# Sums of the way back's weights formed during the way in of a two-layer MLP, and the first loads of the way back asked for earlier

## The chip, the cores and the metric

The kernel runs on one core of one Trainium2 chip. The metric is the device time of one execution in microseconds; the number compared is the median of several executions.

## The reference

Two blocks work on a sequence of 1024 tokens of width 1024, in float32. The first has a mixer, an MLP and a gated addition; the second has a gated MLP, attention beside a state-space mixer, and a second gated MLP. What matters here are the three MLPs:

```python
# first block, MLP: 1024 -> 4096 -> 1024
z = rms_norm(h, norm_mlp_g[l])
h = h + jnp.square(jax.nn.relu(z @ w_up[l])) @ w_down[l]
# second block, twice: 1024 -> 2 x 2816, gated, -> 1024
def swiglu(x, w_in, w_out):
    gate, up = jnp.split(x @ w_in, 2, axis=-1)
    return (jax.nn.silu(gate) * up) @ w_out
```

## The kernel before, in words

**Products.** Each large product is made by Strassen's scheme in Winograd's form: both factors are cut into 2x2 blocks, and seven products of sums of blocks replace eight. Each factor of such a product is split into a float32r high part and a low part (on ScalarE the high part, on VectorE or GpSimd the low one), and three matmuls (high by high, high by low, low by high) stand for one.

**The way in** (`ups_s`, L526 to L606) makes z times the first weight. It goes over pairs of column pieces, numbered n: 16 pairs in the MLP, 22 in each gated one. z's right-hand factors are kept in SBUF as 28 tiles of the tag `u`, which has 32 buffers. A pair's left factors are made by `lefts` (L493 to L517): two `raw` loads of 512 KB, sums on VectorE (L505, L506, L507, L515), splits by `factor`. The pool `raw` (L306) has two buffers, and its loads are kept in program order (`last_raw`, L309 to L311), all on SyncE's queue. For n from 3 on the loop L593 to L604 runs the products p2(n), p3(n-1), p1(n), p4(n-1), asks for the left factors of n+1 (L599), calls `also`, and runs p6(n), p5(n), p7(n); one product is 12 matmuls of 128x512. `use` takes finished quarters through the nonlinearity, and `lay_by` (L608 to L624) forms the sums of h that the way back needs as its left factors and stores them in DRAM (`hs`). The tag `s`, four buffers, holds `st` of `lefts`, and in the MLP also the tiles `hz` and `hw` of `lay_by`.

**The way back** (`down_s`, L645 to L767) makes h times the second weight. It goes over units (p, q): p is one of seven products in the order 2, 1, 5, 3, 6, 7, 4, and q a quarter of the inner dimension (8 of them in the MLP, 6 in the gated ones, the last one half as large). A unit (L691) loads a left factor `sd` from `hs` and a right factor, splits both (L687, L688) into tiles `wh`, `wl`, `tt`, and runs 24 matmuls (L701). A load is put in the schedule behind the end of the unit four units back (`ends`, L661).

**Right factors.** Four of the seven right factors are sums of blocks of the second weight. In the two gated MLPs `rights` (L626 to L637) forms them during the way in: two `raw` loads (`x`, `y`), four subtractions on VectorE (L635), two stores to `tw` in DRAM (L637); the way back loads them from there (`td`). `also` (L1171) spreads the 11 calls over 19 steps. In the MLP there is no `tw`: `right` (L664) loads blocks of `w_down` (`wd`), 64 loads of 512 KB, eight of them a second block for p = 7, and subtracts in place on VectorE (L669) before the split, for p = 5, 6, 7 and 4; the first block stays in the `u` pool (`W`) over several products.

**What sets the order.** Each engine, and SyncE's queue of loads and stores, runs its instructions in the order that the compiler's scheduler wrote down. `after` (L299) adds an ordering to that scheduler alone, without a semaphore. A queue entry that waits holds up all behind it. `aside` hangs other work on given units of the way back: the constants and eighths of the state-space mixer (`s5_small`, `s5_eighth`) and, on unit (7, 4), `ple_in` (L999), which loads the input of the next stage into `raw`. `fetch` (L342) loads the next stage's weights through the same two `raw` buffers.

Of the kernel before, what the change touches and what calls it, by code (L numbers as in the profile page):

```python
# [15 lines left out]
ALU = mybir.AluOpType  # L16
PSUM = bass.MemoryType.PSUM
DRAM = bass.MemoryType.DRAM
P = 128
# [3 lines left out]
H = 512  # L23
# [224 lines left out]
class Model:  # L248
    def __init__(self, ctx, tc, a, out):
        self.tc, self.nc, self.a, self.out = tc, tc.nc, a, out  # L250
        pool = lambda n, b, **k: ctx.enter_context(tc.tile_pool(name=n, bufs=b, **k))
        self.pc = pool("c", 1)
        self.pu = pool("u", 32)
        self.pw = pool("w", NW)
        self.pr = pool("r", 2)
        self.pt = pool("t", 5)
        self.psm = pool("sm", 8)
        self.pd = pool("d", 1, space=DRAM)
        self.last_raw = None
        self.ps = pool("ps", 8, space=PSUM)  # L260


# [79 lines left out]
    def fetch(self, src, k):  # L342
        nc = self.nc
        n = src.shape[-1]
        r = self.raw(src, [n])
        shape = [P, k, n // k] if k else [P, n]
        h = self.pw.tile(shape, F32R, name="wh", tag="wh")
        l = self.pw.tile(shape, F32R, name="wl", tag="wl")
        if k:
            r = r.rearrange("p (k f) -> p k f", k=k)  # L350
        nc.scalar.activation(h, r, AF.Copy)  # L351
        nc.gpsimd.tensor_tensor(l, r, h.bitcast(F32), op=ALU.subtract)  # L352
        return h, l
# [169 lines left out]
        self.pairs = pairs  # L523
        self.first = [self.left_first(pairs[n][0]) for n in range(self.EARLY)]

    def ups_s(self, z, use, also=None):  # L526

        nc = self.nc
        pairs, E = self.pairs, self.EARLY
        left, a, c, s2, s3 = dict(enumerate(self.first)), {}, {}, {}, {}

        def product(p, n, bank, start):
            for k in range(4):
                zh, zl = z(p, k)
                wh, wl = left[n][p][0][:, k, :], left[n][p][1][:, k, :]
                for i, (w, x) in enumerate(((wh, zh), (wh, zl), (wl, zh))):  # L540
                    self.mark = nc.tensor.matmul(bank, w, x, start=start and k == 0 and i == 0,  # L541
                                                 stop=k == 3 and i == 2, skip_group_check=True)

        def p2(n):
            b = c[n] = self.bank()
            product(2, n, b, True)

        def p1(n):
            a[n] = self.bank()
            product(1, n, a[n], True)  # L550
            self.late = self.mark
            s1 = self.tmp("s1c")
            nc.scalar.activation(s1, a[n], AF.Copy)
            use(n, (0, 0), c.pop(n), s1)

        def p5(n):
            c[n] = self.bank()
            product(5, n, c[n], True)

        def p6(n):  # L560
            product(6, n, a[n], False)
            s2[n] = self.pr.tile([P, 2, H], F32, name="s2", tag="xr")[:, 0]
            nc.scalar.activation(s2[n], a[n], AF.Copy)

        def p7(n):
            product(7, n, a[n], False)
            s3 = self.tmp("s3")
            nc.scalar.activation(s3, a[n], AF.Copy)
            use(n, (1, 1), c[n], s3)

        def p3(n):
            product(3, n, c[n], False)
            use(n, (0, 1), c[n], s2[n])

        def p4(n):
            product(4, n, a[n], False)
            use(n, (1, 0), a[n], None)
            for x in (left, a, c, s2):
                del x[n]

        z.ready(0)
        z.settle()
        for n in range(E):
            p2(n)
            p1(n)
        z.ready(1)
        for n in range(E):
            self.lefts(*pairs[n], left[n])
        left[E] = self.lefts(*pairs[E])
        for p, n in ((p5, 0), (p5, 1), (p6, 0), (p6, 1), (p7, 0), (p7, 1), (p3, 0), (p5, 2), (p4, 0), (p6, 2), (p3, 1),  # L590
                     (p7, 2), (p4, 1)):
            p(n)
        for n in range(E, len(pairs)):  # L593
            p2(n)
            p3(n - 1)
            p1(n)
            p4(n - 1)
            if n + 1 < len(pairs):
                left[n + 1] = self.lefts(*pairs[n + 1])  # L599
            if also:  # L600
                also(n - E, len(pairs) - E)
            p6(n)
            p5(n)
            p7(n)  # L604
        p3(n)
        p4(n)  # L606
# [19 lines left out]
    def rights(self, w, tw, d):  # L626
# [9 lines left out]
        for i, t in enumerate((x, y)):  # L636
            nc.sync.dma_start(out=tw[d // 2][2 * i : 2 * i + 2, d % 2].rearrange("i p f -> p i f"), in_=t)  # L637


    RIGHT = {5: 0, 7: 1, 4: 2, 6: 3}  # L640


    LEFT = {2: (0, 0), 1: (0, 1), 5: (1, 0), 3: (1, 1), 6: (2, 0), 7: (2, 1), 4: (3, 0)}

    def down_s(self, hs, w, Y, done, z=None, aside={}, tail=1, tw=None):  # L645

# [1 line left out]
        v = nc.vector  # L650
        npair = w.shape[1]
        qs = [(p, min(2, npair - p)) for p in range(0, npair, 2)]
        W = {}
        ends = [self.late]
        ahead = 4

        def load(name, src, q):
            n = qs[q][1]
            t = self.u(name, shape=[P, 2, H])
            d = nc.sync.dma_start(out=t[:, :n], in_=src.rearrange("c p f -> p c f"))  # L660
            self.after(d, ends[max(len(ends) - ahead, 0)])  # L661
            return t

        def right(p, q):  # L664
            k, n = qs[q]
            if tw and p in self.RIGHT:
                return load("td", tw[q][self.RIGHT[p], :n], q)
            block = lambda b: load("wd", w[b, k : k + n], q)
            sub = lambda o, x, y: v.tensor_tensor(o[:, :n], x[:, :n], y[:, :n], op=ALU.subtract)  # L669
            t = block({2: 2, 1: 0, 5: 1, 3: 3, 6: 3, 7: 3, 4: 2}[p])  # L670
            if tw or p in (2, 3):
                return t
            if p == 1:
                W[q] = t
            elif p in (5, 6):
                sub(W[q], t, W[q])
                return W[q]
            elif p == 7:
                sub(t, t, block(1))
            else:  # L680
                sub(t, t, W.pop(q))
            return t

        def pair(tags, x, n):
            hi, lo = (self.u("tt", F32R, [P, 2, H]) if tag == "u" else self.pw.tile([P, 2, H], F32R, name=tag, tag=tag)
                      for tag in tags)
            nc.scalar.activation(hi[:, :n], x[:, :n], AF.Copy)  # L687
            v.tensor_tensor(lo[:, :n], x[:, :n], hi.bitcast(F32)[:, :n], op=ALU.subtract)  # L688
            return hi, lo

        def unit(p, q):  # L691
            n = qs[q][1]
            g, i = self.LEFT[p]
            s = load("sd", hs[q][g][i, :n], q)
            return pair(("wh", "wl"), s, n), pair(("u", "u"), right(p, q), n)

        def mm(bank, un, c, t, start, stop):
            (sh, sl), (th, tl) = un
# [50 lines left out]
        b = four()  # L749
# [3 lines left out]
        c = four()  # L753
# [11 lines left out]
                z.ready(0)  # L765

        product(4, a, False, c21, rest)  # L767


    def pool_in(self, g, pp):  # L770
# [196 lines left out]
    def mlp(self, z, aside={}):  # L967
        nc = self.nc
        hs, xy = [], {}

        def use(n, quarter, bank, other):
            i, j = quarter
            if (n, j) not in xy:
                xy[n, j] = self.u("h", shape=[P, 2, H], tag="s" if (n, j) == (1, 1) else "u")
            o = xy[n, j][:, (1 - i) if j == 0 else i]
            if other is not None:
                nc.vector.tensor_tensor(o, bank, other, op=ALU.add)
                bank = o
            nc.scalar.activation(o, bank, AF.Relu)
            nc.scalar.activation(o, o, AF.Square)  # L980
            if quarter == (1, 0):
                self.lay_by(hs, n, xy.pop((n, 0)), xy.pop((n, 1)), "s")

        self.ups_s(z, use)
        Y = [None] * NT

        def first(t):
            r = self.raw(self.xm[t], name="xr", tag="xr", after=self.mark)
            nc.vector.tensor_tensor(Y[t], Y[t], r, op=ALU.add)
            return self.rstd(Y[t])  # L990

        done, z = self.follow("norm_ple_g", first, lambda t, r: (Y[t], r))
        aside = dict(aside)
        aside[7, 4] = [self.ple_in]
        self.down_s(hs, self.a["w_down"], Y, done, z, aside)
        self.resume()
        return Y, z

# [148 lines left out]
    def ffn(self, n, z, seam, aside={}):  # L1147
# [19 lines left out]
                self.lay_by(hs, d, X.pop((d, 0)), X.pop((d, 1)), "u")  # L1167

        w, tw = self.a["f%d_out" % n], []

        def also(k, of):  # L1171
            if (k + 1) * w.shape[1] // of > k * w.shape[1] // of:
                self.rights(w, tw, k * w.shape[1] // of)

        self.ups_s(z, use, also)
        Y = [None] * NT
        done, z = seam(Y)
        self.down_s(hs, w, Y, done, z, aside, 1 if z else 2, tw)
        return z

    def half_scale(self, row, name):
# [548 lines left out]
```

## Time and profile before

| | us |
|---|---|
| median of three executions | 3058.43 |
| lowest and highest | 3047.64, 3059.11 |
| the profiled execution, its own time | 3056.01 |
| its span, first to last instruction | 3054.2 |
| TensorE busy (matmuls) | 2828.5 |
| VectorE, ScalarE, GpSimd busy | 1797.1, 1320.1, 784.1 |

The times below are microseconds from the span's first instruction. PE is TensorE, DVE VectorE, ACT ScalarE, POOL GpSimd, and SP SyncE, whose queue issues the loads and stores (SPq). L701 is line 701 of the kernel. In a timeline a bracket gives the engine's idle time before the instruction and what ended it. PEclk is the share of TensorE's full clock that was granted: 1.00 is 2.4 GHz, half of it 1.2 GHz. Matmuls overlap, so one of 0.39 us follows the one before it after less than that.

### The profile page before, as it was taken

How to read it: one execution, taken by the hardware profiler on the slowest of the kernel's cores; microseconds unless marked ns; L12 is line 12 of the kernel's file. 1: busy time of each engine (PE TensorE's matmuls, PEld its weight loads, DVE VectorE, ACT ScalarE, POOL GpSimd, SP SyncE). 2: the span in 40 equal slices, each digit the busy share in tenths (PEclk: the TensorE clock that was granted, in tenths of full speed). 3: DMA queues.
4: the chain of work that ended last, by engine and by line, in shares of the span. 5: the costliest groups of instructions: out<-in, count | busy, mean ns of one | idle time of the engine just before them, and what ended most of it. 6: DMA issues, size and time to landing. Idle time of an engine off the chain costs nothing. (4 is left out here: it accounts for less than half of the span.)

```text
span 3054.2 us, 33886 instructions
## 1 busy us (share of the span) xinstructions
PE 2828.5 (93%) x12585; PEld 2303.4 (75%) x12585; DVE 1797.1 (59%) x2561; ACT 1320.1 (43%) x1921; POOL 784.1 (26%) x626
## 2 busy tenths in 40 slices
PE   8998999989979989999989999997789999998997
PEld 7777877767757867778777878886677778777776
DVE  4586655575767366666667561417735756565445
ACT  5446554442335473323324362236655533332343
POOL 3320222200211221111122041349854112111001
PEclk9999999999989999999999999999899899999999
DMA  4114344474466123454466562423113244446645
GB/s 145 57 47 138 131 145 152 156 259 160 166 233 220 56 90 106 153 164 151 164 222 237 207 222 81 155 83 111 42 49 131 87 152 159 159 153 207 225 160 200
DMA packets 198200, 452.93 MB, mean 148 GB/s; under 512 B 20533, under 2 KB 25233, under 8 KB 198033
## 3 DMA queue, kind: packets, MB, share of 16 engines
q1 hardware_dynamic: 193424, 433.97, 41.9%
q10 hardware_dynamic: 4608, 16.78, 1.4%
q8 instruction: 99, 1.62, 0.2%
q14 instruction: 69, 0.56, 0.1%
HBM read 316.51 MB, written 129.99 MB: 146 GB/s over the span
## 5 line engine op out<-in xcount | busy, mean ns | idle before, releaser
L701 PE MATMUL b<-tt,wh 128*128 128x512 f32 x2128 | 686.2, 403 | 74.0 <-ACT tt L687 64.4
L541 PE MATMUL b<-zh,wh 128*128 128x512 f32 x1680 | 646.9, 398 | 35.4 <-ACT wh L481 25.6
L541 PE MATMUL b<-zh,wl 128*128 128x512 f32 x1680 | 625.3, 393 | 4.5 <-ACT wl L511 4.0
L541 PE MATMUL b<-zl,wh 128*128 128x512 f32 x1560 | 615.2, 395 | 8.4 <-DVE zl L211 8.4
L701 PEld LDWEIGHTS b<-tt,wh 128*128 128x128 f32 x2128 | 409.3, 194 | 181.5 <-ACT tt L687 73.8
L701 PE MATMUL b<-tt,wl 128*128 128x512 f32 x1064 | 424.1, 399 | 0.0
L541 PEld LDWEIGHTS b<-zh,wh 128*128 128x128 f32 x1680 | 319.8, 191 | 123.9 <-ACT wh L481 38.8
L541 PEld LDWEIGHTS b<-zh,wl 128*128 128x128 f32 x1680 | 318.2, 190 | 75.5 <-ACT wl L511 6.7
L541 PEld LDWEIGHTS b<-zl,wh 128*128 128x128 f32 x1560 | 296.4, 190 | 73.9 <-DVE zl L211 13.4
L688 DVE TENSOR_TENSOR wl<-sd,wh 128x1024 fp32r<-128x1024 f32 x140 | 167.6, 1197 | 190.3 <-ACT wh L687 190.3
L482 POOL TENSOR_TENSOR wl<-raw,wh 128x1024 fp32r<-128x1024 f32 x51 | 123.3, 2418 | 526.1 <-ACT wh L481 486.6
L701 PEld LDWEIGHTS b<-tt,wl 128*128 128x128 f32 x1064 | 206.7, 194 | 43.6
L481 ACT ACTIVATE wh<-raw 128x1024 fp32r<-128x1024 f32 x120 | 127.2, 1060 | 238.4 <-DMA raw<-in_f_in 95.2
L352 POOL TENSOR_TENSOR wl<-raw,wh 128x1024 fp32r<-128x1024 f32 (+1 forms) x58 | 142.7, 2465 | 322.0 <-ACT wh L351 290.2
L687 ACT ACTIVATE wh<-sd 128x1024 fp32r<-128x1024 f32 x140 | 141.5, 1011 | 154.6 <-DMA sd<-hs 111.9
L383 POOL TENSOR_SCALAR v<-ss 128x1 f32<-128x1 f32 x80 | 47.9, 599 | 472.5 <-ACT junk L376 466.3
L619 POOL TENSOR_TENSOR hw<-h 128x512 f32<-128x512 f32 x38 | 60.2, 1583 | 421.1 <-DVE h L1165 188.1
L687 ACT ACTIVATE tt<-wd 128x1024 fp32r<-128x1024 f32 x92 | 94.6, 1028 | 150.3 <-DVE wd L669 133.1
L505 DVE TENSOR_TENSOR s<-raw 128x512 f32<-128x512 f32 x60 | 82.2, 1370 | 107.5 <-DMA raw<-in_f_in 100.6
L482 DVE TENSOR_TENSOR wl<-raw,wh 128x1024 fp32r<-128x1024 f32 x69 | 88.7, 1286 | 84.2 <-ACT wh L481 43.2
L351 ACT ACTIVATE wh<-raw 128x1024 fp32r<-128x1024 f32 (+1 forms) x58 | 59.5, 1031 | 168.2 <-issue 42.7
L688 DVE TENSOR_TENSOR tt<-wd,tt 128x1024 fp32r<-128x1024 f32 x92 | 110.2, 1198 | 27.6 <-ACT tt L687 26.8
(358 smaller groups left out, 5003.4 us busy)
## 6 DMA issues: line engine op xcount, KB each, us to landing
sd<-hs SPq DMA_DIRECT2D x126, 512.0 KB, 5.5
raw<-in_f_in SPq DMA_DIRECT2D x94, 512.0 KB, 3.7
wd<-in_w_down SPq DMA_DIRECT2D x64, 512.0 KB, 6.3
raw<-in_f_out SPq DMA_DIRECT2D x44, 512.0 KB, 3.6
tw<-raw SPq DMA_DIRECT2D x44, 512.0 KB, 2.9
td<-tw SPq DMA_DIRECT2D x40, 512.0 KB, 6.3
hs<-h SPq DMA_DIRECT2D x38, 512.0 KB, 3.1
hs<-hw SPq DMA_DIRECT2D x38, 512.0 KB, 3.0
```

The source lines that it names most:

```text
L351: nc.scalar.activation(h, r, AF.Copy)
L352: nc.gpsimd.tensor_tensor(l, r, h.bitcast(F32), op=ALU.subtract)
L383: nc.gpsimd.tensor_scalar(out=v, in0=ss, scalar1=1.0 / D, scalar2=EPS, op0=ALU.mult, op1=ALU.add)
L481: nc.scalar.activation(hi.rearrange("p a b -> p (a b)"), x, AF.Copy)
L482: eng.tensor_tensor(lo.rearrange("p a b -> p (a b)"), x, hi.bitcast(F32).rearrange("p a b -> p (a b)"), op=ALU.subtract)
L505: v.tensor_tensor(s1, a21, a22, op=ALU.add)
L541: self.mark = nc.tensor.matmul(bank, w, x, start=start and k == 0 and i == 0, stop=k == 3 and i == 2, skip_group_check=True)
L619: g.tensor_tensor(wt[:, 1], x[:, 1], y[:, 0], op=ALU.subtract)
L687: nc.scalar.activation(hi[:, :n], x[:, :n], AF.Copy)
L688: v.tensor_tensor(lo[:, :n], x[:, :n], hi.bitcast(F32)[:, :n], op=ALU.subtract)
L701: self.mark = nc.tensor.matmul(bank, x[:, c, ts], y[:, c], start=start and k == 0, stop=stop and k == 2, skip_group_check=True)
```

## The change

- The MLP gets `rights` too. `back` makes the hooks for all three MLPs: `also` now has all the sums done one step before the last (`of - 1`), so 16 calls over 12 steps in the MLP and 11 over 18 in the gated ones, and `down_s` has no other path: its right factors are `td` or an unchanged block `wd`.
- `last`, called once in the last pair behind p1(n), asks for the factors of units (2, 0) to (2, 3), eight tiles of the tag `u`, which `unit` then takes from `self.pre`.
- `fetch` is put in the schedule behind `self.gate`, the end of the fifth unit from the end of the way back that came last (unit (4, 3) in the MLP, (4, 1) in the first gated one).
- `ple_in` moves from unit (7, 4) to (7, 2).

```diff
@@ -342,7 +342,7 @@
     def fetch(self, src, k):
-        r = self.raw(src, [n])
+        r = self.raw(src, [n], after=self.gate)
@@ -594,11 +594,12 @@
             p2(n)
             p3(n - 1)
             p1(n)
+            if n + 1 == len(pairs):
+                last()
             p4(n - 1)
             if n + 1 < len(pairs):
                 left[n + 1] = self.lefts(*pairs[n + 1])
-            if also:
-                also(n - E, len(pairs) - E)
+            also(n - E, len(pairs) - E)
@@ -636,13 +637,34 @@
+    def back(self, hs, w, tw):
+        n = w.shape[1]
+        def also(k, of):
+            for d in range(k * n // (of - 1), min((k + 1) * n // (of - 1), n)):
+                self.rights(w, tw, d)
+        def last():
+            self.pre = []
+            for q in range(4):
+                g, i = self.LEFT[2]
+                pair = []
+                for name, src in (("sd", hs[q][g][i]), ("wd", w[2, 2 * q : 2 * q + 2])):
+                    t = self.u(name, shape=[P, 2, H])
+                    self.after(self.nc.sync.dma_start(out=t, in_=src.rearrange("c p f -> p c f")), self.mark)
+                    pair.append(t)
+                self.pre.append(pair)
+        return also, last
@@ -650,35 +672,13 @@
-        W = {}
-        ends = [self.late]
+        ends = []
         ahead = 4
...
-            self.after(d, ends[max(len(ends) - ahead, 0)])
-            return t
-        def right(p, q):
-            k, n = qs[q]
-            if tw and p in self.RIGHT:
-                return load("td", tw[q][self.RIGHT[p], :n], q)
-            block = lambda b: load("wd", w[b, k : k + n], q)
-            sub = lambda o, x, y: v.tensor_tensor(o[:, :n], x[:, :n], y[:, :n], op=ALU.subtract)
-            t = block({2: 2, 1: 0, 5: 1, 3: 3, 6: 3, 7: 3, 4: 2}[p])
...
+            self.after(d, ends[len(ends) - ahead])
             return t
@@ -689,10 +689,14 @@
         def unit(p, q):
-            n = qs[q][1]
-            g, i = self.LEFT[p]
-            s = load("sd", hs[q][g][i, :n], q)
-            return pair(("wh", "wl"), s, n), pair(("u", "u"), right(p, q), n)
+            k, n = qs[q]
+            if self.pre:
+                x, y = self.pre.pop(0)
+            else:
+                g, i = self.LEFT[p]
+                x = load("sd", hs[q][g][i, :n], n)
+                y = load("td", tw[q][self.RIGHT[p], :n] if p in self.RIGHT else w[{2: 2, 1: 0, 3: 3}[p], k : k + n], n)
+            return pair(("wh", "wl"), x, n), pair(("u", "u"), y, n)
@@ -765,6 +769,7 @@
         product(4, a, False, c21, rest)
+        self.gate = ends[-5]
@@ -981,7 +986,8 @@
-        self.ups_s(z, use)
+        w, tw = self.a["w_down"], []
+        self.ups_s(z, use, *self.back(hs, w, tw))
@@ -991,8 +997,8 @@
-        aside[7, 4] = [self.ple_in]
-        self.down_s(hs, self.a["w_down"], Y, done, z, aside)
+        aside[7, 2] = [self.ple_in]
+        self.down_s(hs, w, tw, Y, done, z, aside)
@@ -1167,15 +1173,10 @@
-        def also(k, of):
-            if (k + 1) * w.shape[1] // of > k * w.shape[1] // of:
-                self.rights(w, tw, k * w.shape[1] // of)
-        self.ups_s(z, use, also)
+        self.ups_s(z, use, *self.back(hs, w, tw))
```

## Rows read from the trace of the kernel before

**Rows 1.** Stages: us, busy PE PEld DVE ACT POOL, PEclk, DMA share, GB/s.

```profile
290.00:602.70 312.70, 298.73 (x1276) 240.96 (x1276) 186.42 (x197) 161.20 (x239) 81.72 (x43) 0.98 0.41 140
602.70:986.00 383.30, 337.65 (x1446) 268.25 (x1447) 266.89 (x462) 150.71 (x173) 47.74 (x77) 0.94 0.59 208
...
2808.50:3054.20 245.70, 217.31 (x924) 176.50 (x924) 120.92 (x116) 94.51 (x116) 18.05 (x18) 0.95 0.58 204
```

**Rows 2.** PE's timeline in the way in, two matmuls eleven steps apart.

```profile
584.80 0.39 PE L541 MATMUL b<-zh,wh 128*128 128x512 f32 x1
...
587.30 0.39 PE L541 MATMUL b<-zh,wl 128*128 128x512 f32 x1
```

**Rows 3.** PE's waits in the MLP's way back: in total, times, longest.

```profile
PE b L701 <- ACT tt L687: 41.0, 16, 7.7
PE b L701 <- DVE tt L688: 4.1, 5, 1.9
```

**Rows 4.** PE's timeline: units of the MLP's way back that started late.

```profile
604.99 0.50 PE L701 MATMUL b<-tt,wh 128*128 128x512 f32 x1 [2.31 <-ACT tt L687]
621.74 0.80 PE L701 MATMUL b<-tt,wh 128*128 128x512 f32 x1 [3.98 <-ACT tt L687]
662.10 0.79 PE L701 MATMUL b<-tt,wh 128*128 128x512 f32 x1 [5.54 <-ACT tt L687]
916.90 0.80 PE L701 MATMUL b<-tt,wh 128*128 128x512 f32 x1 [7.71 <-ACT tt L687]
```

**Rows 5.** The subtraction at L669: ns min/median/max, first and last start.

```profile
L669 DVE TENSOR_TENSOR wd<-wd x32: 1206/1218/3420, 687.8 to 973.0; 128x1024 f32<-128x1024 f32 x32
```

**Rows 6.** SP's queue in the MLP's way back, ahead of two of those units.

```profile
654.36 0.34 SPq L1310 DMA_DIRECT2D sxy<-sxb  x1
...
891.50 1.70 SPq L307 DMA_DIRECT2D raw<-in_pT  x2
906.65 0.33 SPq L307 DMA_DIRECT2D raw<-in_w_proj  x1
907.08 0.38 SPq L660 DMA_DIRECT2D sd<-hs  x1
```

**Rows 7.** PE's timeline: the first matmul of each gated MLP's way back.

```profile
1573.45 0.80 PE L701 MATMUL b<-tt,wh 128*128 128x512 f32 x1 [7.26 <-ACT tt L687]
...
2814.14 0.79 PE L701 MATMUL b<-tt,wh 128*128 128x512 f32 x1 [5.66 <-ACT tt L687]
```

**Rows 8.** SP's queue, first gated MLP: left factors, sums, left factors; first way-back load.

```profile
1309.78 2.90 SPq L307 DMA_DIRECT2D raw<-in_f_in  x2
1320.20 2.82 SPq L307 DMA_DIRECT2D raw<-in_f_out  x2
...
1329.96 2.48 SPq L307 DMA_DIRECT2D raw<-in_f_in  x2
...
1564.64 0.54 SPq L660 DMA_DIRECT2D sd<-hs  x1
```

**Rows 9.** SP's queue in the MLP's way in: first loads of four pairs.

```profile
359.36 1.14 SPq L307 DMA_DIRECT2D raw<-in_w_up  x1
...
477.87 0.35 SPq L307 DMA_DIRECT2D raw<-in_w_up  x1
...
498.71 0.34 SPq L307 DMA_DIRECT2D raw<-in_w_up  x1
...
558.99 0.35 SPq L307 DMA_DIRECT2D raw<-in_w_up  x1
```

**Rows 10.** Loads through the raw buffers, both ways in: KB, median us to landing.

```profile
raw<-in_w_up SPq DMA_DIRECT2D x29, 512.0 KB, 4.7
...
raw<-in_f_out SPq DMA_DIRECT2D x22, 512.0 KB, 3.7
```

**Rows 11.** Sums on DVE: ns min/median/max; L635 gated MLP, L506 MLP, ways in.

```profile
L635 DVE TENSOR_TENSOR raw<-raw x44: 678/692/694, 1214.9 to 1559.1; 128x512 f32<-128x512 f32 x44
...
L506 DVE TENSOR_TENSOR st<-s,raw x15: 678/1777/1780, 295.2 to 575.0; 128x512 f32<-128x512 f32 x15
```

More of the change, by code (lines that the diff above doesn't have):

```diff
@@ L258, in __init__ @@
         self.pd = pool("d", 1, space=DRAM)
-        self.last_raw = None
+        self.last_raw = self.gate = None
         self.ps = pool("ps", 8, space=PSUM)
@@ L524, in open_s, with ups_s @@
         self.first = [self.left_first(pairs[n][0]) for n in range(self.EARLY)]
-    def ups_s(self, z, use, also=None):
+    def ups_s(self, z, use, also, last):
         nc = self.nc
@@ L550, in p1 @@
             product(1, n, a[n], True)
-            self.late = self.mark
             s1 = self.tmp("s1c")
@@ L637, in rights, with down_s @@
             nc.sync.dma_start(out=tw[d // 2][2 * i : 2 * i + 2, d % 2].rearrange("i p f -> p i f"), in_=t)
+    def back(self, hs, w, tw):
[14 more added lines that the diff above has]
+        return also, last
     RIGHT = {5: 0, 7: 1, 4: 2, 6: 3}
     LEFT = {2: (0, 0), 1: (0, 1), 5: (1, 0), 3: (1, 1), 6: (2, 0), 7: (2, 1), 4: (3, 0)}
-    def down_s(self, hs, w, Y, done, z=None, aside={}, tail=1, tw=None):
+    def down_s(self, hs, w, tw, Y, done, z=None, aside={}, tail=1):
         nc = self.nc
@@ L652, in down_s, with load @@
         qs = [(p, min(2, npair - p)) for p in range(0, npair, 2)]
-        W = {}
-        ends = [self.late]
+        ends = []
         ahead = 4
-        def load(name, src, q):
-            n = qs[q][1]
+        def load(name, src, n):
             t = self.u(name, shape=[P, 2, H])
             d = nc.sync.dma_start(out=t[:, :n], in_=src.rearrange("c p f -> p c f"))
-            self.after(d, ends[max(len(ends) - ahead, 0)])
-            return t
-        def right(p, q):
-            k, n = qs[q]
-            if tw and p in self.RIGHT:
-                return load("td", tw[q][self.RIGHT[p], :n], q)
-            block = lambda b: load("wd", w[b, k : k + n], q)
-            sub = lambda o, x, y: v.tensor_tensor(o[:, :n], x[:, :n], y[:, :n], op=ALU.subtract)
-            t = block({2: 2, 1: 0, 5: 1, 3: 3, 6: 3, 7: 3, 4: 2}[p])
[L671 to L681, printed above, removed]
+            self.after(d, ends[len(ends) - ahead])
             return t
@@ L691, in unit @@
         def unit(p, q):
-            n = qs[q][1]
-            g, i = self.LEFT[p]
-            s = load("sd", hs[q][g][i, :n], q)
-            return pair(("wh", "wl"), s, n), pair(("u", "u"), right(p, q), n)
+            k, n = qs[q]
[6 more added lines that the diff above has]
+            return pair(("wh", "wl"), x, n), pair(("u", "u"), y, n)
         def mm(bank, un, c, t, start, stop):
@@ L1169, in ffn @@
         w, tw = self.a["f%d_out" % n], []
-        def also(k, of):
-            if (k + 1) * w.shape[1] // of > k * w.shape[1] // of:
-                self.rights(w, tw, k * w.shape[1] // of)
-        self.ups_s(z, use, also)
+        self.ups_s(z, use, *self.back(hs, w, tw))
         Y = [None] * NT
         done, z = seam(Y)
-        self.down_s(hs, w, Y, done, z, aside, 1 if z else 2, tw)
+        self.down_s(hs, w, tw, Y, done, z, aside, 1 if z else 2)
         return z
```

## The prediction

> **What bounds the kernel now.** I read the page first: PE is busy for 93% of the span, so a stage is paid for by what PE waits for and by the clock it then gets. Next I cut the span into stages [rows 1]: the MLP's way in (290 to 602.7), its way back (602.7 to 986), and, as a way back with little else in it, the one of the second gated MLP (from 2808.5). Back to back, matmuls follow each other at (587.30 - 584.80) / 11 = 0.227 us [rows 2], so a product of the way in (12 matmuls) takes 2.72 us, a pair (7 products) 19.1 and a unit of the way back (24) 5.45. The MLP's way back has 56 units, 305 us of such matmuls, in a stretch of 383.3. Of the 78 us left over, 45.1 are PE's waits for the split factors [rows 3]. About 10 are, by my estimate, the small matmuls of the state-space parts (1446 - 1344, at about 0.1). The remaining 23 are slow matmuls: the granted clock is 0.94 of the full 2.4 GHz on the mean of this stage and 0.98 in the way in [rows 1], and 6% of 383.3 is 23.
>
> Then I asked which units started late [rows 4]. The first ones (2.31 and 3.98) wait for loads asked for at the seam. The one at 662.10 (5.54) follows a queue held up on SP until 654.36, where a store waits for the state-space constants [rows 6]. The other 13 waits for ACT, 41.0 - 2.31 - 3.98 - 5.54 = 29.2 together, lie among or after the subtractions at L669, the first at 687.8 [rows 5]. The longest, 7.71, has another cause besides: after the loads of `pT`, SP stood still from 891.50 + 1.70 to 906.65, since the next stage's weights needed a `raw` buffer, and the unit's own loads came behind [rows 6].
>
> In the gated MLPs the way back starts 7.26 and 5.66 late [rows 7]; the first load was issued at 1564.64, 9 us ahead of the first matmul [rows 8].
>
> The ways in have little to give on PE, but one resource is full: the two `raw` buffers. In the MLP the next pair's first load is issued 498.71 - 477.87 = 20.8 us after the last one [rows 9], one pair's time: each buffer is asked for again as soon as it comes free.
>
> **The change part by part.**
>
> *Way back of the MLP.* 32 subtractions of 1.22 us [rows 5] leave DVE, 39 us, and each leaves the chain load, subtraction, split. Eight loads of 512 KB go (64 `wd` become 24 `wd` and 32 `td`), and the `W` tiles no longer hold `u` buffers. Of the 29.2 us of waits I take 22 as gone: those that follow L669, and the 7.71, as the gate keeps the weights from standing in SP's queue there. Kept are about 7, at the seams between products and behind the state-space work on DVE. The clock: fewer stalls leave fewer slow matmuls, and about half of the 23 us, 12, comes back (not all: the other way back, with no subtractions, still has 0.95 [rows 1]). `ple_in` two units earlier issues the same two loads and splits 11 us sooner, beside matmuls: nothing; without that cover it would cost two loads' landing once.
>
> *First four units.* Their eight loads are issued behind p1 of the last pair. p2 and p1 have then read their eight tiles of z for the last time, so the `u` buffers are there. About six products (16 us) remain, and the loads need the 9 us seen today. In the gated MLPs 7.26 + 5.66 = 12.9 us go, and with them some slow matmuls, an estimated 1.5 at each seam from the stage's clock: 16. What is late next are the seams between products. Past them on SP are only the last stores of `hs`, which wait for DVE and POOL as before. In the MLP 2.31 + 3.98 go as well, but the constants that held SP until 654.36 take as long as ever, so PE comes to the unit at 662.10 earlier and waits there longer: I count 2 of the 6.3.
>
> *Weights held back.* Loads that stood finished in `raw` come some 20 us before the end of the way back instead. Both their splits and the stage that uses them come later than that: nothing. If they came too late, one landing and one split would show, 5 us.
>
> *Way in of the MLP: sums moved in.* 16 calls add 32 loads, 64 subtractions on halves, 32 stores, all through the two `raw` buffers in program order with the left factors. PE does not see the subtractions (64 x 0.692 = 44 us [rows 11], on a DVE that is busy 186 of 312.7 [rows 1]); it sees the buffers. Their price is read in the gated MLP: left factors hold them 1320.20 - 1309.78 = 10.4 us, sums 1329.96 - 1320.20 = 9.8 [rows 8]. One call fits into a pair (20.2 against 19 to 20), but four of the twelve steps have two. Between the first load of the sixth pair (359.36) and that of the last (558.99) lie the left factors of ten pairs, and now 14 calls: 10 x 10.4 + 14 x 9.8 = 241 us instead of 199.6, so the last pair's load goes out 41.6 us later. But today PE has a backlog: from that load to the end of the way in are 43.7 us, while the landing (4.7 [rows 10]), a split and nine products (24.5) need 30.3. That slack of 13.4 is used up first. Cost: 41.6 - 13.4 = 28.
>
> The bounds: if the ring can run ahead in the first pairs, or packs tighter, it is near 0. If it is looser, every link counts: the MLP's loads land in 4.7 us against 3.7 [rows 10], as its stores of `hs` share the queues, and 1 us on each of the 24 links makes 52. I take 28, since the row with both kinds of load in it is the nearest.
>
> A page speaks against this move. In the MLP, sums on DVE take 1777 ns where POOL works beside them and 678 alone, while L635 in the gated MLPs never passed 694 [rows 11]. The Trainium skill, SBUF — State Buffer, "SBUF: two separate sides", says that DVE with two SBUF inputs and GpSimd lock one port pair for a whole instruction. By that rule the sums pay here as L506 does: POOL is busy 81.7 of 312.7 [rows 1], two sums of a call lie on the ring, so 28 x 0.26 x 1.1 = 8 us on top; by the rows of L635 nothing. I leave it out of the sum; the bound of 52 covers it.
>
> *Gated ways in.* The calls move by less than a step, as many as before: nothing, covered by buffers idle part of the time; uncovered it is one call, 10 us.
>
> *Sum.* 28 - (22 + 12 + 2) - 16 = -24. The profiled execution took 3056.0 (its span and 1.8 around it), 2.4 below the median of 3058.4, against which results will stand: 3058.4 - 24 = 3034.
>
> **The rivals.**
>
> *The ring is held by the order on DVE: slower.* In the MLP, left factors today hold the buffers for 20.8 us, not 10.4 [rows 9]: L506 stands on DVE behind `lay_by` of the pair before and takes 1777 ns there [rows 11]. If the scheduler keeps that order, the sums come in series behind it: 10 x 20.8 + 14 x 9.8 = 345 instead of 199.6, less 13.4, is +132 on the way in, and with the gains of 52 the kernel takes 3138. For it: the order in the trace, and four buffers of tag `s` as before. Against: L506 may stand so late only because nothing pressed; with the buffers late PE can run p3 and p4 of the pair before first. It decides where a pair's share of the ring passes (199.6 + 13.4 + 52) / 10 = 26.5 us (the forecast has 24.1): from there the way in costs more than the 52 that the rest brings. Half way from the forecast to it is 3086.
>
> *The ring costs about what the rest brings: no change.* The loose bound of 52 gives 3058.
>
> *The ways in hide all of it: faster still.* Then 3058 - 52 = 3006. Against it: buffers that are never free today.
>
> *The early asks do nothing.* SP issues in order; if the eight loads stand behind the last stores after all, the 16 us of the gated seams stay, and the sum is -8: 3050.
>
> **How the numbers follow.** Forecast (3015 to 3043): 0.36; hidden: 0.10; no change, from the loose ring: 0.17; early asks without effect: 0.06; ring held by the order: 0.31, spread from 3074 to 3138. A measurement of this kernel can tell 0.5% (15 us) from no change. Faster by more than that: 0.36 + 0.10 = 0.46; within it: 0.23; slower: 0.31. The likeliest case's own range is 3015 to 3043. The range for 8 in 10 leaves out the best half of the hidden case (0.05) and the worse half of the held ring (0.15): 3003 to 3106.
>
> **What would show it.** Right: in the MLP's way back no L669, PE's waits for ACT near 13 us instead of 41.0, granted clock 0.96 or more; at both gated seams a first matmul with under 1 us of idle time; SP without a hole at `w_proj`. In the MLP's way in: `raw` loads back to back, left factors 10 to 11 us and sums about 10, the stage about 28 us longer, with PE waiting for L481 at every third pair. Wrong: L506 still behind `lay_by` with first loads of two pairs over 26.5 us apart on the mean; or the MLP's way back as long as before, which would mean that state-space work on DVE and SP's queue, not the subtractions, set its pace; or seams as late as now.

## The result, and the profile after

The changed kernel takes 3088.22 us, the median of four executions (3087.49 to 3092.33), against 3058.77 of the kernel before (3047.64 to 3059.50, four): the ratio is 1.0108, with a 95% interval of 1.0083 to 1.0132. It is slower by 1.1%, where 0.8% faster was forecast. The profiled execution has a span of 3086.3 us against 3054.2, 32.1 more.

The stages of [rows 1] in the trace of the changed kernel (us, busy PE, PEld, DVE, ACT, POOL, granted clock, DMA share, GB/s): the MLP's way in, its way back, and the second gated way back.

```profile
290.00:675.40 385.40, 318.47 (x1277) 252.53 (x1278) 226.57 (x264) 166.30 (x245) 78.59 (x43) 0.90 0.60 206
675.40:1011.50 336.10, 320.55 (x1447) 262.27 (x1446) 222.38 (x428) 143.31 (x166) 52.52 (x77) 0.98 0.63 219
2839.70:3086.30 246.60, 217.44 (x925) 176.59 (x923) 115.64 (x112) 86.24 (x108) 19.14 (x18) 0.94 0.54 186
```

Against [rows 1] the way in is 72.7 us longer (312.7 to 385.4), the way back 47.2 shorter (383.3 to 336.1), and all that follows 6.6 longer (2068.2 to 2074.8). These three make the 32.1; the second gated way back is as long as before (245.7, 246.6). On the way in PE is busy 19.7 us longer for the same matmuls, with the granted clock down from 0.98 to 0.90, and idle 53 us longer. Most of that idle time is one wait, for the high part of a left factor. PE's waits on the way in (total, times, longest):

```profile
PE b L542 <- ACT wh L481: 41.3, 8, 12.6
PE b L542 <- ACT s L563: 6.2, 4, 4.7
PE b L542 <- ACT s1c L553: 5.0, 3, 3.2
```

The same wait was 6.5 us before. Behind it stands the ring of the two `raw` buffers, here on SP's queue from one call to the next, the counterpart of [rows 9]:

```profile
359.08 0.37 SPq L307 DMA_DIRECT2D raw<-in_w_down  x1
...
440.18 0.38 SPq L307 DMA_DIRECT2D raw<-in_w_down  x1
...
442.76 0.38 SPq L307 DMA_DIRECT2D raw<-in_w_down  x1
...
447.63 1.81 SPq L638 DMA_DIRECT2D tw<-raw  x2
450.43 1.83 SPq L307 DMA_DIRECT2D raw<-in_w_up  x2
...
460.73 5.80 SPq L307 DMA_DIRECT2D raw<-in_w_down  x2
...
470.81 2.29 SPq L638 DMA_DIRECT2D tw<-raw  x2
473.58 2.88 SPq L307 DMA_DIRECT2D raw<-in_w_up  x2
...
485.56 0.37 SPq L307 DMA_DIRECT2D raw<-in_w_down  x1
...
634.78 2.10 SPq L307 DMA_DIRECT2D raw<-in_w_up  x2
```

Of the 61 loads through `raw` in this way in, 56 waited for the last reader of their buffer, on DVE, or for the landing of a store from it (SP's waits: total, times, longest):

```profile
SPq L307 <- DVE raw L515: 87.9, 13, 12.8
SPq L307 <- DVE wl L482: 40.7, 15, 5.7
SPq L307 <- DMA tw<-raw: 37.8, 28, 3.1
```

From one user's first load to the next user's first load is a link of the ring, the time for which the user holds it: a call here takes 450.43 - 440.18 = 10.3 us, the left factors 10.3, the next call 12.9. Over the whole stretch of the forecast, from 359.08 to the last pair's first load at 634.78, the 14 calls take 11.5 us on the mean (9.4 to 13.1) and the ten left factors 11.4 (9.9 to 14.3).

On the way back the subtractions are gone. PE's waits there, for [rows 3]:

```profile
PE b L705 <- ACT tt L687: 14.1, 3, 7.1
PE b L705 <- DVE tt L688: 1.5, 2, 1.1
```

At the first gated seam, in place of the 7.26 us of [rows 7], PE waits 3.04 us in the last products of the way in and 4.13 us at the second group of the way back (the 0.69 between them stood there before too, as 0.75 us):

```profile
1580.97 0.80 PE L542 MATMUL b<-zh,wh 128*128 128x512 f32 x1 [3.04 <-ACT s L563]
1587.15 0.51 PE L542 MATMUL b<-zh,wh 128*128 128x512 f32 x1 [0.69 <-ACT s L568]
1597.91 0.80 PE L705 MATMUL b<-tt,wh 128*128 128x512 f32 x1 [4.13 <-DVE tt L688]
```

ACT and DVE around these two waits:

```profile
1579.38 1.06 ACT L687 ACTIVATE wh<-sd 128x1024 fp32r<-128x1024 f32 x1 [2.36 <-DMA sd<-hs]
1580.34 0.58 ACT L563 ACTIVATE s<-b 128x512 f32<-128x512 f32 x1
...
1594.36 0.69 DVE L619 TENSOR_TENSOR hz<-h 128x512 f32<-128x512 f32 x1
1595.09 1.63 DVE L621 TENSOR_TENSOR hw<-hz,h 128x512 f32<-128x512 f32 x1
1596.65 5.69 DVE L688 TENSOR_TENSOR tt<-wd,tt 128x1024 fp32r<-128x1024 f32 x4
```

The first unit of the way back now starts without a wait. But ACT stands at an early split that still waits for its load, with an eviction behind it that the way in needs; and DVE forms the low parts of the right factors only behind `lay_by` of the last pair. The second gated seam shows the same (2.64, 0.69 and 4.13 us).

### The profile page after: what moved, and what is told of

It reads as the page before. It is cut to its first block, busy times and chain, and to the rows that moved or that the text cites. A ratio compares the mean times of both kernels' runs of the same rounds, so it can differ in the third digit from the quotient of the medians.

```text
span 3086.3 us, 34045 instructions
## 1 busy us (share of the span) xinstructions
PE 2837.0 (92%) x12585; PEld 2312.7 (75%) x12585; DVE 1794.2 (58%) x2593; ACT 1317.1 (43%) x1921; POOL 788.3 (26%) x626
## 5 line engine op out<-in xcount | busy, mean ns | idle before, releaser
L542 PE MATMUL b<-zh,wh 128*128 128x512 f32 x1680 | 658.0, 405 | 89.1 <-ACT wh L481 55.3
L705 PE MATMUL b<-tt,wh 128*128 128x512 f32 x2128 | 674.7, 397 | 39.3 <-ACT tt L687 24.6
L542 PE MATMUL b<-zh,wl 128*128 128x512 f32 x1680 | 632.1, 397 | 7.0 <-ACT wl L511 6.8
L542 PE MATMUL b<-zl,wh 128*128 128x512 f32 x1560 | 623.2, 400 | 8.9 <-DVE zl L211 8.9
L542 PEld LDWEIGHTS b<-zh,wh 128*128 128x128 f32 x1680 | 325.0, 194 | 184.5 <-ACT wh L481 67.5
L542 PEld LDWEIGHTS b<-zh,wl 128*128 128x128 f32 x1680 | 321.7, 192 | 80.3 <-ACT wl L511 10.4
L542 PEld LDWEIGHTS b<-zl,wh 128*128 128x128 f32 x1560 | 301.8, 193 | 75.1 <-DVE zl L211 13.3
L505 DVE TENSOR_TENSOR s<-raw 128x512 f32<-128x512 f32 x60 | 86.8, 1447 | 152.7 <-DMA raw<-in_f_in 101.9
L636 DVE TENSOR_TENSOR raw<-raw 128x512 f32<-128x512 f32 x152 | 107.2, 705 | 102.3 <-DMA raw<-in_w_down 60.1
L688 DVE TENSOR_TENSOR tt<-td,tt 128x1024 fp32r<-128x1024 f32 x128 | 151.5, 1183 | 22.1 <-ACT tt L687 21.3
L687 ACT ACTIVATE tt<-td 128x1024 fp32r<-128x1024 f32 x128 | 128.7, 1006 | 28.6 <-DMA td<-tw 18.2
```

The costliest lines, as they stand in the source:

```text
L505: v.tensor_tensor(s1, a21, a22, op=ALU.add)
L636: nc.vector.tensor_tensor(o, p, q, op=ALU.subtract)
L705: self.mark = nc.tensor.matmul(bank, x[:, c, ts], y[:, c], start=start and k == 0, stop=stop and k == 2, skip_group_check=True)
```

## The experiments

Lengths of the two MLP stages in each trace, cut at the same places as above (the way in from 22.7 us behind its first matmul), and of what follows up to the end of the span. Each ratio is to runs of the kernel before made beside it (their medians lie between 3056.7 and 3060.8 us), so small differences between kernels are read from the ratios and not from the medians:

| kernel | way in | way back | rest | median us | ratio to before (95%) |
|---|---|---|---|---|---|
| before | 312.7 | 383.3 | 2068.2 | 3058.77 | 1 |
| changed | 385.4 | 336.1 | 2074.8 | 3088.22 | 1.0108 (1.0083 to 1.0132) |
| e1 own buffers | 321.1 | 336.1 | 2076.9 | 3059.94 | 1.0002 (0.9993 to 1.0011) |
| e2 sums back | 311.8 | 364.1 | 2076.0 | 3044.08 | 0.9956 (0.9942 to 0.9970) |
| e3 one call a step | 358.5 | 338.5 | 2076.6 | 3070.10 | 1.0035 (1.0022 to 1.0047) |
| e4 no early asks | 379.9 | 352.0 | 2073.2 | 3097.03 | 1.0122 (1.0109 to 1.0136) |
| e5 own buffers, held | 329.9 | 336.5 | 2073.5 | 3032.88 | 0.9935 (0.9917 to 0.9952) |
| e6 e5, two units early | 333.7 | 345.9 | 2081.3 | 3051.57 | 0.9982 (0.9972 to 0.9993) |
| e7 no held weights | 382.2 | 348.5 | 2076.7 | 3090.14 | 1.0120 (1.0104 to 1.0137) |
| e8 sums out of place | 360.3 | 337.6 | 2076.5 | 3062.69 | 1.0023 (1.0013 to 1.0033) |
| e9 e5, seam order | 328.1 | 342.7 | 2082.3 | 3037.10 | 0.9924 (0.9909 to 0.9939) |
| e10 e5, one call a step | 315.9 | 345.3 | 2079.4 | 3035.97 | 0.9927 (0.9912 to 0.9943) |
| e11 e5, early in MLP only | 331.5 | 337.0 | 2073.5 | 3036.05 | 0.9931 (0.9918 to 0.9945) |
| e12 e5, from the start | 326.4 | 337.3 | 2076.3 | 3031.99 | 0.9913 (0.9898 to 0.9928) |

**e1, buffers of their own.** Nothing holds the tags `g` and `dg` during the MLP's way in. The edit is for the MLP alone; the gated MLPs keep `raw`.

```diff
-        x, y = (self.raw(w[b : b + 2, d].rearrange("b p f -> p b f"), [2, H]) for b in (0, 2))
+        x, y = (self.u("raw", shape=[P, 2, H], tag=tag) for tag in ("g", "dg"))
+        for t, b in ((x, 0), (y, 2)):
+            nc.sync.dma_start(out=t, in_=w[b : b + 2, d].rearrange("b p f -> p b f"))
```

> The changed kernel, but in the MLP the right-factor sums are formed in two buffers of their own (tags g and dg, which nothing holds in that stage) instead of the two raw buffers; same loads, same 64 subtractions, same stores. Theory R (the two raw buffers alone make the way in 73 us longer: left factors and sums pass through them one after the other, some 80 us for three left factors and four calls): the way in falls from 383 to 310-318 us, PE's waits for wh L481 there fall from 41 us to under 8, the way back stays near 336, the kernel takes 3010-3022 us. Rival D (DVE's extra 44 us and its order, whatever the buffers): the way in stays above 360, the kernel above 3065. Rival M (64 more transfers slow all landings): raw loads land in 6 us or more in place of 4.7 and the way in stays above 340, the kernel above 3045.

The way in fell to 321.1 us, but the kernel gained only 28, as the way in began 31 us later: free of the order of `raw`, loads and subtractions of the sums were scheduled into the first mixer, the first subtraction at 165.8 us, and its matmuls waited (11.34 us at 200.81, 9.56 at 222.66). So this run could not tell R from D, since only 15 of the 64 subtractions were left in the way in; e5 mends that.

**e2, the sums on the way back again** (`also` does nothing in the MLP; `right` and its subtractions return).

> The changed kernel, but the MLP's right-factor sums are formed on the way back again, as in the kernel before; early asks, held weights and the earlier ple_in stay. Theory R: the way in returns to 308-314 us; the way back goes from 336 to 375-381 (before 383, less the first units' 2.31 and 3.98 us), as most of the 47 us gained there come from the sums; the kernel takes 3050-3062 us. Rival G (the gain on the way back comes from the early asks and the held weights more than from the sums): the way back stays below 355 and the kernel below 3035. Rival D' (the way in is longer through the early asks, not the sums): the way in stays above 340.

R holds on the way in (311.8). The way back took 364.1, halfway between R and G: the sums are worth 364.1 - 336.1 = 28 us there, and 19 of the gain come from the other parts. These parts alone make a kernel faster than before, by 0.44%.

**e3, one call a step**, 12 calls instead of 16; the last two quarters q of the MLP subtract on the way back.

```diff
-            for d in range(k * n // (of - 1), min((k + 1) * n // (of - 1), n)):
+            for d in (range(k, min(k + 1, 12)) if n == 16 else ...):
```

> The changed kernel with 12 calls instead of 16 in the MLP, one in each step and never two; the last two of the eight double pieces get their sums on the way back, as before the change. By the forecast's prices (left factors 10.4 us, a call 9.8: 20.2 against 19.1 to 20 for a pair) the way in is 310-316 us long, the way back 336 + 10 = 346, the kernel takes 3020-3032 us. By the ring as it stands in the trace of the changed kernel (some 11.6 for the left factors, 11.3 for a call: 22.9 a pair, ten pairs, less 13 of slack) the way in is 333-345 us long and the kernel takes 3044-3058. If double calls cost nothing special (theory: price by the call), e3 lies on the line from before to after: 12/16 of +73, a way in of 360 and more.

The way in was 358.5 us, 42 above the range of the forecast's prices, 13 above the second one and near the third (three quarters of the calls, 63% of the 72.7): calls of 11.5 us, as in the changed kernel, and left factors of 12.6 make 24.1 a pair, not 20.2. So the steps with two calls are not the main cause: without any of them 45.8 of the 72.7 us stay, and any call is too dear for this ring. The 12 calls brought nearly all of the gain on the way back (338.5).

**e4, no early asks** (`last` asks for nothing; `ends` begins with `self.late` again).

> The changed kernel without the early asks: the first four units' factors are loaded at the seam again, in all three MLPs. Theory W (at the gated seams the wait only changed its place: 4.13 us at the second group of matmuls for DVE's split, 3.0 us and more in the last products of the way in for evictions that stand on ACT behind a split that waits for its load): both gated seams take 7 and 6 us again, the ends of the ways in lose 3 us each, the MLP's seam takes 4-6 us again; the kernel within 6 us of the changed one, 3084-3096. Rival F (the forecast: early asks give 16 us, something else took them): the kernel at 3100 or more. Rival N (early asks cost more than they bring): 3080 or less.

PE's first late matmuls at the three seams:

```profile
677.36 1.22 PE L706 MATMUL b<-tt,wh 128*128 128x512 f32 x2 [6.37 <-ACT tt L688]
...
694.23 1.22 PE L706 MATMUL b<-tt,wh 128*128 128x512 f32 x2 [2.86 <-ACT tt L688]
...
1603.02 1.22 PE L706 MATMUL b<-tt,wh 128*128 128x512 f32 x2 [5.88 <-ACT tt L688]
...
2854.84 1.65 PE L706 MATMUL b<-tt,wh 128*128 128x512 f32 x3 [5.61 <-ACT tt L688]
```

W holds at the gated seams: at the first one 0.75 + 5.88 us, against 3.04 + 0.69 + 4.13 with early asks, and all that follows the MLP takes 2073.2 against 2074.8. The early asks earn what they earn in the MLP, where both stages together take 731.9 us without them and 721.5 with them. The intervals of the two kernels' ratios overlap, so this 10 rests on the profiles.

**e5, own buffers, held.** As e1, but each load of a sum is put in the schedule behind the step's last matmul.

```diff
+                self.after(nc.sync.dma_start(out=t, in_=...), self.mark)
```

> As e1, but each load of the sums is held in the scheduler's order behind the last matmul issued in its step, so that it can't be pulled ahead into the first mixer, as it was in e1 (there sums stood in SP's queue from 200 us on, and the way in began 30 us later than in the changed kernel). Theory R (the two raw buffers alone): the first mixer as in the changed kernel, the MLP's way in from 292 us on 310-322 us long in place of 383, its way back 334-338; the kernel takes 3012-3026 us. Rival D (the subtractions on DVE, in whatever buffers): with all 64 inside the way in again it is 350 us or longer and the kernel above 3055.

```profile
290.00:619.90 329.90, 305.20 (x1277) 246.80 (x1278) 231.74 (x269) 165.91 (x245) 82.25 (x43) 0.95 0.71 247
619.90:956.40 336.50, 321.53 (x1447) 263.56 (x1446) 219.27 (x424) 142.81 (x165) 53.10 (x77) 0.97 0.60 214
```

All 64 subtractions are in the way in again (DVE is busy 231.74 us of a shorter stretch), and 55.5 of its 72.7 extra us are gone. D falls; the ring was the main cause. (The sums leave the two buffers and the program order of `raw` loads at once here; e8 keeps the order.) The 17.2 that stay are more than R allowed (322 us), and the kernel (3032.88) is above R's 3026, so the ring is not quite all. It is 0.65% faster than before.

**e6, two units early** (`range(2)` in `last`).

> As e5, but the early asks take two units instead of four, so that of the eight u buffers free by then four are left for the right factors' splits of these units, and SP has four loads less ahead of it. Theory U (at the gated seams the splits of the right factors stand behind lay_by on DVE because their buffers come free last; and eight loads at once land late, so that splits hold up evictions on ACT): the waits of 4.13 us at the second group of matmuls and of 3.0 us at p6 or p7 go, 4-10 us in all against e5: 3004-3018. Rival E (the seam waits for the last evictions and lay_by, whatever is loaded): within 3 us of e5.

Neither came: it is 19 us slower than e5. Both gated seams kept their waits (3.29 and 4.13, 3.37 and 4.13), so the buffers were not what put DVE's splits late, and in the MLP the third unit now waited 5.68 us for its load. What made the rest of the 19 us, 7.8 of them behind the MLP, stays open.

**e7, no held weights** (`after=self.gate` gone, `ple_in` on (7, 4)).

> The changed kernel without the held weights and with ple_in two units later, as before the change: the next stage's weights may stand in SP's queue during a way back again. Theory Q: the unit behind ple_in is late by about 7.7 us again, nothing else moves: the MLP's way back 342-345 instead of 336, the kernel 3092-3100. Rival N: without the sums on DVE the late unit is hidden: the kernel within 3 us of the changed one, 3085-3091. Rival L: held weights come late at the next stage: 3084 or less.

The late unit is back, behind the same entry of SP's queue as in [rows 6]:

```profile
944.88 0.33 SPq L307 DMA_DIRECT2D raw<-in_w_proj  x1
945.26 0.43 SPq L680 DMA_DIRECT2D sd<-hs  x1
```

```profile
953.27 1.22 PE L705 MATMUL b<-tt,wh 128*128 128x512 f32 x2 [7.18 <-ACT tt L687]
```

The trace says Q: the way back is 12.4 us longer. But the profiled execution, 3100.52 us, was the slowest of the five; the median is only 2 above the changed kernel's, so the sum of it stays between Q and N.

**e8, sums out of place.** The loads still pass through `raw`; the results go to `g` and `dg` and are stored from there.

```diff
+        a, b = (self.u("tw", shape=[P, 2, H], tag=tag) for tag in ("g", "dg"))
-        for o, p, q in ((x[:, 0], x[:, 1], x[:, 0]), (x[:, 1], y[:, 1], x[:, 1]), ...
+        for o, p, q in ((a[:, 0], x[:, 1], x[:, 0]), (a[:, 1], y[:, 1], x[:, 1]), ...
```

> The changed kernel, but in the MLP the sums are written to two other buffers (tags g and dg) and stored from there: the loads still pass through raw in the same order, but raw is free after the last subtraction and not after the store has landed. By the links of the changed kernel (a call holds the ring for 11.5 us on the mean, of which some 3.3 are the store's issue and landing): a call holds it for 7.5-8.5, from the sixth pair's first load to the last's 10 x 11.4 + 14 x 8 = 226 us instead of 275, the way in is 325-340 us long, the kernel takes 3030-3047. Rival K (the links are set by SP's order or by the transfers' share of the queues, not by who holds the buffer): call links stay above 10.5 us, the way in above 365, the kernel above 3070.

The calls did as expected, 8.5 us each over the same stretch of 14 calls, so who holds the buffers does set the links. But the left factors then held the ring for 13.3 on the mean instead of 11.4, and the way in was 360.3 us long, between the two theories. What they lost stands in the DMA issues of that stretch (KB, median us to landing), first of the changed kernel, then of e8:

```profile
raw<-in_w_down SPq DMA_DIRECT2D x28, 512.0 KB, 3.9
tw<-raw SPq DMA_DIRECT2D x28, 512.0 KB, 3.0
raw<-in_w_up SPq DMA_DIRECT2D x22, 512.0 KB, 4.2
```

```profile
raw<-in_w_down SPq DMA_DIRECT2D x28, 512.0 KB, 3.9
tw<-tw SPq DMA_DIRECT2D x28, 512.0 KB, 4.1
raw<-in_w_up SPq DMA_DIRECT2D x22, 512.0 KB, 5.9
```

The left factors' loads now run beside the stores that they used to wait for, and land 1.7 us later, about the 1.9 by which their links grew.

**e9, the order at the seams.** On e5: the early units' splits on ACT stand behind p7's eviction of the last pair, and the low parts of their right factors are formed on POOL.

> As e5, with the order of the early units' splits changed: on ACT they stand behind the last eviction that the way in waits for (p7's copy of the last pair), and the right factors' low parts of these four units are formed on POOL instead of DVE, where lay_by stands before them. Theory V (the early asks bring the data in time, and their gain at the gated seams is eaten by the order of the splits: 3.0 to 3.8 us each at the last evictions, 4.13 at DVE's split): the waits of 3 us at L542 go at all three seams, those of 4.13 at the second group shrink below 2; the kernel 8-18 us faster than e5, 3015-3025. Rival E (splits that are done later only make the way back start later): L542 waits go but the first matmuls of the way back wait 4 us or more; within 4 us of e5, 3029-3037.

The waits at L542 shrank to 0.7 or 0.8 each, and the way back paid for it (PE, then POOL, at the first gated seam):

```profile
1540.43 0.73 PE L713 MATMUL b<-tt,wh 128*128 128x512 f32 x2 [2.52 <-ACT tt L692]
...
1546.67 0.79 PE L713 MATMUL b<-tt,wh 128*128 128x512 f32 x1 [5.04 <-POOL tt L695]
```

```profile
1542.16 1.71 POOL L620 TENSOR_TENSOR hw<-h 128x512 f32<-128x512 f32 x1 [28.73 <-DVE h L1179]
1543.83 2.79 POOL L695 TENSOR_TENSOR tt<-wd,tt 128x1024 fp32r<-128x1024 f32 x1
```

E holds: POOL too has `lay_by` ahead of the split, and needs 2.79 us where DVE needs 1.2. By the ratios the kernel can't be told from e5 (0.9924 and 0.9935, each inside the other's interval).

**e10, one call a step** on e5, and **e12, from the start**: all 16 calls, four of them beside the first three pairs.

> As e5, with 12 calls instead of 16, one a step (as e3 against the changed kernel). e3's way back was only 2.4 us longer than the changed kernel's with all 16 calls. Theory P (in e5 the way in is still 15 us longer than before because the double calls' loads and stores share the queues with the left factors' loads): the way in falls to 312-318 us from 292 on, the way back 336-339; the kernel 3020-3028. Rival C (every call costs PE about 1 us by its DVE time and its transfers): way in 322-326, the kernel 3028-3036.

> As e5 and e10: all 16 calls in buffers of their own, but four of them already beside the first three pairs of the way in (one after every third product there) and then one a step. Theory P (it is the double calls that cost e5's way in 14 us against e10's): the way in is 339-345 us long from its first matmul (e5 352.9, e10 338.9), the way back 335-338 (e5 336.1, e10 344.9); the kernel 3018-3027. Rival C (every call in the way in costs PE about 1 us wherever it stands, or DVE has no room beside the first pairs, where the splits of z are): way in 350 or more, the kernel within 4 us of e5, 3029-3040.

With 12 calls in buffers of their own the way in is only 3.2 us longer than before (315.9, as P has it); the way back lost 9 (345.3), which e3 had not let expect, and the kernel is at 3036, where C had it. In e12 the way in took 326.4 (349.1 from its first matmul, where P had 339 to 345), the kernel 3031.99. So 12 calls cost 3 us and four more another 10 to 14, wherever they stand; why was not found. e12 has the lowest ratio of all, 0.9913; those of e9 and e10 lie inside its interval, those of e5 and e11 just above.

**e11, early asks in the MLP only**, on e5.

> As e5, with the early asks in the MLP alone; both gated MLPs load their first units at the seam again. Theory W (at the gated seams early asks only move the wait): gated seams 6 us and 5.6 us again, the 3.0 and 2.6 us at the last evictions and the 4.13 gone; the kernel within 5 us of e5, 3028-3038. Rival F (they gain as forecast): 3045 or more.

W again: the gated seams wait 5.50 and 5.54 us, the rest takes 2073.5 us with or without the early asks, the kernel is within 4 us of e5. Where the time goes shows from stage to stage: with early asks (e5) the two gated ways in are 5.1 and 2.9 us longer than here, and the seams with the ways back behind them 5.1 and 3.7 shorter.

## Why the prediction was wrong

The forecast had -24 us and the profiled executions +32.1, a miss of 56: 44.7 in the MLP's way in and 22.6 behind the MLP, where 16 were to be gained, less 11.2 on its way back. That 3088 us lie between the forecast's 3003 and 3106 is luck: the range reached so far up for a rival whose mechanism is not what happened.

- **Way in of the MLP, +28: wrong, +72.7. This is the step that failed**, by its size. The mechanism, sums and left factors one after the other through two buffers, is borne out by e5. Two numbers in it were off. The links: 10 x 10.4 + 14 x 9.8 = 241 us was measured as 634.78 - 359.08 = 275.7, 34.7 more (11.4 us for left factors, 11.5 for a call). I had priced them from one call and one set of left factors [rows 8], called the nearest because both kinds stand in it; it was among the fastest of its kind. In the same trace the next left factors take 11.4 and 12.2 us (first loads at 1329.96 [rows 8], 1341.40, 1353.57), and of the eight calls from 1250.84 to 1493.34 six take 16 to 19, as the second load waits for its buffer:

```profile
1341.40 0.34 SPq L307 DMA_DIRECT2D raw<-in_f_in  x1
...
1353.57 8.75 SPq L307 DMA_DIRECT2D raw<-in_f_out  x2
...
1369.52 3.35 SPq L307 DMA_DIRECT2D raw<-in_f_in  x2
```

The slack: I let the backlog shrink the stretch after the last load from 43.7 us to 30.3; it took 675.4 - 634.78 = 40.6. PE still had 144 matmuls left there, not 108, and waited 5.4 us for evictions on ACT, 4.7 of them for one behind an early split. 34.7 + 10.3 is the 45 that was missing. The bound of 52 failed as well: it put 1 us on each of 24 links, which took 1.44, and kept the whole slack.
- **The order on DVE as the holder of the ring: right to doubt it as a mechanism.** `lay_by` is now done before the left factors' load has landed (DVE stood idle 50.7 us for these loads ahead of L505), L506 follows L505 by 1.2 to 3.7 us from the sixth pair on, in place of some 8, and no longer takes 1777 ns [rows 11]; the first loads of two pairs are (634.78 - 370.62) / 10 = 26.4 us apart, close to the rival's 26.5, but from the price of the links.
- **The sums on DVE beside POOL, left out of the sum: right.** The three lines in the way in, ns min/median/max, for [rows 11]:

```profile
L505 DVE TENSOR_TENSOR s<-raw x15: 677/1610/2098, 293.7 to 640.9; 128x512 f32<-128x512 f32 x15
...
L506 DVE TENSOR_TENSOR st<-s,raw x15: 675/679/686, 294.9 to 644.3; 128x512 f32<-128x512 f32 x15
...
L636 DVE TENSOR_TENSOR raw<-raw x61: 679/692/1657, 363.6 to 666.2; 128x512 f32<-128x512 f32 x61
```

The sums take 692 ns in the median, as in the gated MLPs, and 713 on the mean: (0.713 - 0.692) x 61 = 1.3 us more in all. The Trainium skill, SBUF — State Buffer, "SBUF: two separate sides", by which the forecast had priced 8 us, agrees with this trace: the 11 of 15 L505 that begin while POOL splits the pair's other load end 0.55 to 0.58 us behind that split, however long it still ran (alone such an operation takes 0.68). What L506 paid beside POOL's part of `lay_by` (1777 ns before, 11 of 15) it no longer pays, as it does not meet it; L505 went from a median of 1311 ns to 1610. But only 5 of the 61 sums begin while one of POOL's operations runs, where the forecast took POOL's busy share, 0.26, for the share of sums that do.

- **Way back of the MLP, -36: right in kind, too small (-47.2).** Against [rows 1] PE's idle time fell by 30.1 us (45.65 to 15.55) and its busy time by 17.1, at a clock of 0.98 against 0.94; I had 24 and 12. The waits for ACT came to 14.1 us where 13 was forecast. By e2 the sums are 28 of the 47. The first units gave more than the 2 I allowed: 2.31 and 3.98 are gone, and the wait behind the constants did not take them over but shrank (4.37 us at 723.44 in place of 5.54). The unit behind the weights [rows 6] is cured, as e2 and e7 show, but in the changed kernel another one is 7.12 us late at 934.83, because SP waits 8.5 us, until 927.06, for state-space work on DVE (L1372) ahead of the unit's loads.
- **Gated seams, -16: wrong, nothing; a second step that failed, and here by its mechanism.** Loads were not the last thing that the seam waited for. DVE's and POOL's `lay_by` of the last pair stands ahead of the splits, and ACT's early splits stand ahead of evictions. I had written that what is late next are the seams between products and that `hs` stores pass as before; the queue that I did not look into was that of the engines that split. e4 and e11 price the early asks there at zero, e9 shows that another order moves the wait once more.
- **Gated ways in and held weights, nothing:** not contradicted, but from the MLP's end to the end of the span every variant takes 5 to 14 us more than before, with the early asks or without, with the gate or without. e7 and e11 exclude each of these two parts alone; the later `also` of the gated MLPs was not undone, so its share stays open, as does that of the spread between executions. In the changed kernel's trace, counted from first to last matmul, 1.2 and 4.8 us are added in the two gated ways in and 3.0 between the first gated way back and the second way in; 3.1 are saved in the first gated seam and way back.

## What to carry to other kernels

Price a shared ring of buffers by all the links that a trace has of it, under pressure, and not by one tidy sample; and where the new work can have buffers of its own, give it those: the same change is 1.1% slower through the shared ring and 0.7 to 0.9% faster beside it. About half of that gain or more, 0.44%, comes without any moved sums (e2); what the sums add beside the ring is 0.2% in e5, whose interval overlaps e2's, and 0.4% in e12, whose interval does not. Work set free of one order needs another, or the scheduler pulls it to where it hurts (e1). Before loads are asked for earlier, look at what stands ahead of their first user on its own engine's queue: if that is the last work of the stage before, as at the gated seams here, the wait only moves.

## What the runs showed of the hardware

Where a buffer came free earlier, the transfers behind it were slower: in e8 the calls held the ring 3.0 us less, and the left factors' loads, now issued beside the calls' stores, landed in 5.9 us instead of 4.2, and the stores in 4.1 instead of 3.0. That gave back about 19 of the 43 us (ten times 1.9, fourteen times 3.0) that the shorter calls saved. The mean load does not explain it: in e5 the same loads landed in 4.8 us, with the core's DMA engines busier over the way in (0.71 against 0.64). And waits cost twice: the way in's 1277 matmuls kept PE busy for 318.47 us at a mean granted clock of 0.90, against 298.73 at 0.98 before [rows 1], so that beside 53 us of added waiting 20 us of slower matmuls were paid. Last, of VectorE beside GpSimd: in the MLP's way in, the 22 L505 (11 before the change, 11 after) and the 11 L506 (before) that began inside one of POOL's operations all ended 0.54 to 0.58 us behind it and took 0.69 to 2.10 us, so what one pays is what was left of POOL's operation when it began.
